# Layer B of a two-layer encoder: instructions that wait for another engine are issued one background share after their inputs

## The chip, the cores and the metric

The kernel runs on one core of one Trainium2 chip, in one launch. The metric is the device time of the execution in microseconds (us). The engines are PE (TensorE), DVE (VectorE), ACT (ScalarE), POOL (GpSimd) and SP (SyncE, which issues most DMAs). Each works through its own instructions in a fixed order, and the program makes it wait on semaphores for what other engines or DMAs produce.

## What is computed

Two layers run over 2048 prompt frames and 64 sample frames of width 1024:

```python
def gated_attention_layer(x_p, x_s, ck, cv, norm_g, w_in, q_g, k_g, w_out,
                          n_heads, n_kv, past_chunks, bias_fn, sinks):
    qp, kp, vp, gp = project(x_p, norm_g, w_in, q_g, k_g, n_heads, n_kv)
    op = prompt_band_attention(qp, kp, vp, past_chunks, bias_fn, sinks)
    y_p = x_p + (op * jax.nn.silu(gp)) @ w_out
    qs, ks, vs, gs = project(x_s, norm_g, w_in, q_g, k_g, n_heads, n_kv)
    os_, nk, nv = sample_band_attention(qs, ks, vs, ck, cv, bias_fn, sinks)
    y_s = x_s + (os_ * jax.nn.silu(gs)) @ w_out
```

`project` is an RMSNorm, one matrix product that gives queries, keys, values and gate, and an RMSNorm per head of 64 on queries and keys. The band is the own chunk of 64 frames and the past chunks. Layer A has 16 query heads on 2 key/value heads, 2 past chunks and sinks. Layer B has 16 heads, 8 past chunks and a learned bias by clipped distance. The outputs are the two results and the newest keys and values of both layers.

## The kernel before

Layer A takes the first part of the span (to about 690 us), its output projection follows, layer B lies between 876 and 2055 us, and its output projection ends the program. The change is to layer B.

Layer B goes through eight **head pairs**. In each it goes through units of 256 prompt frames (two tiles of 128) and one sample unit of 64. For a tile, `project` (L679 to L681) multiplies the normed input (fp16, in a high and a low part) by the head pair's 512 columns of weights into a PSUM bank `pj`: queries, keys, values and gate. `evacuate_b` takes it out: L715 (ACT) queries and keys into `pa`, L719 (ACT) the high half of the values, L720 (DVE) their low half, L723 (ACT) the gate into `pb`. The sample unit's bank is emptied by `evacuate_sample` (L740).

Then come small steps that change engines, each a **background item** in `bg`: `head_norm` squares (L756, POOL), sums (L757, DVE), adds and takes a power (L760, L761, POOL) and scales (L774, DVE); `gate` takes a tanh (L782, ACT) and multiplies (L783, DVE); `store_kv` scales the keys and stores (L795, POOL and SP). In the kernel before, squares, sums and power are one item, and tanh and product are one.

Attention works on what earlier projections left: queries and keys are transposed into the bank `tp` and taken out in a high half (L1355, L1356, ACT) and a low half (L1367 queries, L1371 keys, DVE); scores go into a bank `sb` (L1416, L1417); L1420 (DVE) adds the bias and takes the row's negative maximum `nm`; L1429 (ACT) is the exponential; L844 transposes the probabilities; L816 (ACT) and L817 (DVE) take them out as high and low half `ph` and `pl`; products (L1526 and L1527 for the sample unit) write the bank `o`. `finish_pairs` takes `o` out: L1247 (ACT) copies one half, L1249 (DVE) adds the other, L1250 (POOL) multiplies by the gate, L1252 (SP) stores.

The scan finds the largest magnitudes of the weights, from which powers of two for the fp16 scales follow: `scan` loads 128 x 512 weights (L182, SP) and reduces the block that it loaded a call before (L175, DVE). At the end of a head pair `across` transposes the maxima through `tp` (L197), and `everywhere` spreads the scales (L213 and the copy behind it). `load_weights` multiplies the weights by the scales (L467 ACT, L470 DVE).

**What sets the order.** PE's order is written out by hand: attention steps come due at marks of the projection's progress (`filler`), so that projection matmuls fill the time in which a step's inputs are made. At each attention step `bg.share` runs a share of the queue of background items, urgent items first. A background item's DVE and ACT instructions are tied behind the latest L1420 and L1429 (`anchor`), and each scan load behind the latest load of inputs (`behind`). The order of DVE, ACT, POOL and SP is otherwise left to the framework's scheduler, which goes by the order in which instructions are emitted and by when it reckons them ready. Banks of PSUM: two `pj`, one `tp`, two `sb`, one `o`.

Of the kernel before, what the change touches and what calls it, by code (L numbers as in the profile page):

```python
# [51 lines left out]
LAG = 4  # L52
HALF = 5 * 2 * P
# [3 lines left out]
def hybrid_encoder_kernel(  # L57
# [114 lines left out]
    def scan(i=None):  # L172
        if pending:
            j, raw = pending.pop()
            nc.vector.tensor_reduce(  # L175
                most[:, j : j + 1], raw, axis=AX.X, op=ALU.max, apply_absolute_value=True
            )
            scanned.append(j)
        if i is not None:
            raw = t("scan", [P, 512], 2)  # L180
# [12 lines left out]

    def across(a, b):
        ps = psum("tp", 512, 1)
# [14 lines left out]
    def everywhere(h, o):  # L210
        ps = psum("tp", 512, 1)
        nc.tensor.matmul(ps[:, 0:3], ones[0:1, 0:1].to_broadcast([1, P]), o, start=True, stop=True)
        nc.vector.tensor_copy(scl[:, h], ps[:, 0:3])  # L213
# [14 lines left out]
    def input_scales(h):  # L228
        everywhere(h, row[:, 20:23])
        nc.vector.tensor_scalar(gsb[:, h], gain[:, 1, :], S_W(h), 1.0, op0=ALU.mult, op1=ALU.mult)  # L230
# [25 lines left out]
    def scale_work(hp, u, e):  # L256
        at = 2 * u + e
        if hp < 7:
            if at < 8:
                scan(8 * (hp + 1) + at)  # L260
            elif at == 8:
                scan()
# [6 lines left out]
            if 11 <= at < 14 and i < 84:  # L269
                scan(i)  # L270
            elif at == 14:
                scan()
# [15 lines left out]
    def bias_vectors_a():  # L288
        oh = held["oh"]
        ps = psum("tp", 512, 1)  # L290
# [79 lines left out]
    class Background:  # L370
        def __init__(self):
            self.queue, self.anchors, self.cost, self.lazy = [], {}, 0.0, False

        def put(self, cost, fn, urgent=False, lazy=False, weights=False):
            it = Item()
            it.fn, it.cost, it.urgent, it.weights = fn, cost, urgent, weights
# [13 lines left out]
        def run(self, it):  # L390
            if it.fn is None:
                return
            fn, it.fn = it.fn, None
# [24 lines left out]
        def share(self, least, parts, few):  # L418
            left = sum(it.weights for it in self.queue)
            self.drain(max(least, self.cost / parts), 1 if left <= few else 2)  # L420

    bg = Background()

    def load_weights(g, *specs, scale=None):
        dt = F32R if scale is None else F16
# [80 lines left out]
    def load_act(  # L506
        src, o, T, squares=False, joint=False, lead=None, cache=None, cached=False, dt=F32R,
        rows=None, scale=None,
    ):
        x = Item()  # L510
# [123 lines left out]
    def token_rows(unit):  # L634
        _, T, tiles = unit
        ps = psum("tp", 512, 1)
# [75 lines left out]
    def evacuate_b(hp, tt, ps, g):  # L712
# [7 lines left out]
        nc.vector.scalar_tensor_tensor(  # L720
            vh[:, :, HD:P], v, c, vh[:, :, 0:HD], op0=ALU.mult, op1=ALU.subtract
        )
# [24 lines left out]
    def head_norm(n, src, spread=True):  # L747
# [3 lines left out]
        def squares():  # L751
            sq = t("sq", [P, 256], 2)
            f.append(t("f", [P, 4], 3))
            fv = f[0][:n, :H]
            if spread:
                nc.gpsimd.tensor_tensor(sq[:n, : H * HD], src, src, op=ALU.mult)  # L756
                nc.vector.tensor_reduce(  # L757
                    fv, sq[:n, : H * HD].rearrange("p (h d) -> p h d", d=HD), axis=AX.X, op=ALU.add
                )
                nc.gpsimd.tensor_tensor(fv, fv, small[:n, :H], op=ALU.add)  # L760
                nc.gpsimd.tensor_tensor(fv, fv, mhalf[:n, :H], op=ALU.pow)  # L761
                return
# [7 lines left out]

        def scale():
# [4 lines left out]
        return [bg.put(0.15 * H, squares, True), bg.put(0.1 * H, scale, True)]  # L776

    def gate(n, g):
        def fn():
            W = g.shape[1]  # L780
            e = t("sq", [P, 256], 2)
            nc.scalar.activation(e[:n, :W], g, AF.Tanh, scale=0.5)  # L782
            nc.vector.scalar_tensor_tensor(g, e[:n, :W], 1.0, g, op0=ALU.add, op1=ALU.mult)  # L783

        return [bg.put(0.3, fn)]
# [6 lines left out]
    def store_kv(layer, rows, kn, v, kdst, vdst):  # L792
# [9 lines left out]
        return bg.put(0.1, fn)  # L802
# [62 lines left out]
    class Filler:  # L865
# [9 lines left out]
        def step(self):  # L875
            if self.gen is None:
# [23 lines left out]
            if not self.attending:  # L900
                bg.drain(FR * c)
# [1027 lines left out]
```

## Time and profile before

| | |
|---|---|
| time, median of 3 runs | 2213.11 us (2212.63 to 2213.92) |
| the profiled execution | 2212.35 us, of it 2210.5 us in the span |
| mean granted clock of PE | 0.987 |
| busy over the span | PE 95%, DVE 70%, ACT 64%, POOL 45% |
| share of the chain that ended last | PE 58%, DVE 15%, DMA 9%, ACT 8%, issue 6%, POOL 4% |

A busy engine is one that executes; in the rest of the span it waits or has nothing to do. In the timeline a row has its start, its duration, engine, line, operation, output and inputs with their shapes, how many instructions it groups, and in brackets the idle time before it with what ended it. A row of waits has the waiting instruction, what it waited for, the total, how often, and the longest.

### The profile page before, as it was taken

The numbers are of one execution on the slowest core, as the hardware profiler recorded it, in microseconds if no ns is written. First come the engines' busy times: TensorE is split into PE (matmuls) and PEld (weight loads), VectorE is DVE, ScalarE is ACT, GpSimd is POOL, SyncE is SP. The second block draws the span as 40 slices with busy tenths as digits, with TensorE's granted clock in tenths as the row PEclk, the third lists the DMA queues.
The fourth block names the chain that finished last, engine by engine and source line by source line (L and its number), as shares of the span: only waits on it lengthen the run. The fifth ranks groups of instructions, "written<-read, shape, count | busy, mean of one in ns | idle before, by whom it ended". The sixth has DMA issues, their size and how long they took to land.

```text
span 2210.5 us, 41329 instructions
## 1 busy us (share of the span) xinstructions
PE 2110.9 (95%) x13441; PEld 1526.6 (69%) x13441; DVE 1547.2 (70%) x4105; ACT 1424.8 (64%) x3610; POOL 999.5 (45%) x1509
## 2 busy tenths in 40 slices
PE   7999999999999999999999989999999999998999
PEld 6877888787889997555555555555555555566888
DVE  6769777677676456787777776777767767577542
ACT  6878878677785333666666766766667667576420
POOL 5645544334355355853444444444444445443000
PEclk9999999999999999999999999999999999999999
DMA  8856546856545667445465565664646556345664
GB/s 276 275 160 215 180 125 220 229 164 182 180 128 178 216 192 256 158 143 172 117 180 136 128 178 133 160 167 115 196 118 162 158 118 171 95 105 136 198 202 124
DMA packets 383096, 372.87 MB, mean 169 GB/s; under 512 B 174672, under 2 KB 320352, under 8 KB 382848
## 3 DMA queue, kind: packets, MB, share of 16 engines
q1 hardware_dynamic: 382880, 370.23, 58.0%
q8 instruction: 106, 1.74, 0.3%
q14 instruction: 110, 0.90, 0.1%
HBM read 257.59 MB, written 73.43 MB: 150 GB/s over the span
## 4 chain that ended last, share of the span: by engine, by line
PE 58%; DVE 15%; DMA 9%; ACT 8%; issue 6%; POOL 4%; SPq 1%; POOLq 0%; ACTq 0%; DVEq 0%
PE pj L679 9%; PE pj L681 9%; PE pj L680 9%; PE pj L1772 4%; PE pj L1774 4%; PE pj L1773 4%; DMA scan<-in_w_in_b_dram 3%; DVE p L1420 3%; PE sb L844 2%; PE sa L844 2%; PE o L1607 2%; PE tp L844 2%; PE o L1568 2%; PE sb L1416 1%; ACT p L1429 1%
## 5 line engine op out<-in xcount | busy, mean ns | idle before, releaser
L679 PE MATMUL pj<-wh,xx 128*128 128x512 f16 (+2 forms) x1648 | 644.6, 391 | 5.2 <-ACT pb L702 3.9
L681 PE MATMUL pj<-wh,xx 128*128 128x512 f16 (+2 forms) x1648 | 626.4, 380 | 2.5 <-POOL xx L564 2.5
L680 PE MATMUL pj<-wh,xx 128*128 128x512 f16 x1024 | 392.0, 383 | 0.0
L1429 ACT ACTIVATE p<-p,nm 128x640 f32<-128x640 f32 (+5 forms) x264 | 199.2, 754 | 202.6 <-DVE nm L1420 102.4
L1772 PE MATMUL pj<-xx,wh 128*128 128x264 f32 (+1 forms) x1024 | 291.4, 285 | 8.0 <-DVE res L1778 2.7
L1773 PE MATMUL pj<-xx,wh 128*128 128x264 f32 (+1 forms) x1024 | 288.8, 282 | 0.0
L680 PE MATMUL pj<-wl,xx 128*128 128x512 f32 (+1 forms) x624 | 234.1, 375 | 2.2 <-DVE wl L470 2.2
L1420 DVE CUSTOM_DVE_ANT_0 p<-sb,BT 128x640 f32<-128x640 f32 (+5 forms) x272 | 195.7, 720 | 44.7 <-PE sb L1417 42.3
L564 POOL TENSOR_TENSOR xx<-xraw,xx 128x528 fp32r<-128x528 f32 (+4 forms) x144 | 183.8, 1295 | 88.9 <-ACT xx L563 82.1
L1464 POOL TENSOR_TENSOR values<-p,values 128x640 f16<-128x640 f32 (+2 forms) x112 | 141.2, 1261 | 159.4 <-ACT values L1463 158.8
L1250 POOL TENSOR_TENSOR o<-gt,o 128x256 f32<-128x256 f32 (+1 forms) x132 | 100.8, 763 | 207.7 <-DVE o L1249 96.8
L761 POOL TENSOR_TENSOR f<-f,mhalf 128x4 f32<-128x4 f32 (+2 forms) x187 | 187.5, 1003 | 13.7
L681 PEld LDWEIGHTS <-xx 128*128 128x128 f16 x1024 | 101.0, 99 | 126.4 <-issue 4.7
L756 POOL TENSOR_TENSOR sq<-pa 128x256 f32<-128x256 f32 (+2 forms) x187 | 113.1, 605 | 147.1 <-ACT pa L715 94.3
L1156 ACT ACTIVATE p<-p,nm 128x257 f32<-128x257 f32 (+2 forms) x272 | 134.3, 497 | 51.1 <-DVE nm L1150 42.9
L774 DVE TENSOR_TENSOR pa<-pa,f 128x256 f32<-128x256 f32 (+3 forms) x221 | 120.3, 544 | 57.9 <-POOL f L761 53.2
L679 PEld LDWEIGHTS <-xx 128*128 128x128 f16 x1024 | 101.3, 99 | 71.9 <-issue 3.1
L680 PEld LDWEIGHTS <-xx 128*128 128x128 f16 x1024 | 101.1, 99 | 70.1 <-issue 3.0
L1774 PE MATMUL pj<-xx,wl 128*128 128x264 f32 x512 | 145.7, 285 | 0.8 <-DVE wl L463 0.8
L1774 PE MATMUL pj<-xx,wh 128*128 128x264 f16 x512 | 142.7, 279 | 2.1 <-DVE wh L460 2.1
L1150 DVE CUSTOM_DVE_ANT_0 p<-sa,BT,nsink 128x256 f32<-128x256 f32 (+2 forms) x272 | 117.4, 467 | 36.0 <-PE sa L844 29.9
L679 PEld LDWEIGHTS pj<-wh,xx 128*128 128x128 f32 x624 | 118.7, 190 | 23.0 <-ACT pb L702 4.8
(273 smaller groups left out, 5276.9 us busy)
## 6 DMA issues: line engine op xcount, KB each, us to landing
xx<-xsb SPq DMA_DIRECT2D x112, 512.0 KB, 4.1
xx<-xsa SPq DMA_DIRECT2D x88, 512.0 KB, 4.8
xraw<-oga SPq DMA_DIRECT2D x64, 264.0 KB, 3.6
xraw<-ogb SPq DMA_DIRECT2D x64, 264.0 KB, 3.7
xsa<-xx SPq DMA_DIRECT2D x32, 512.0 KB, 4.1
scan<-in_w_in_b_dram SPq DMA_DIRECT2D x64, 256.0 KB, 4.5
wl<-in_w_in_b_dram SPq DMA_DIRECT2D x64, 256.0 KB, 4.1
xraw<-in_x_dram SPq DMA_DIRECT2D x40, 256.0 KB, 4.0
```

The lines of the kernel that those rows point to most:

```text
L564: nc.gpsimd.tensor_tensor(lo, rv, wide(hi), op=ALU.subtract)
L679: nc.tensor.matmul(ps[:n, :C], xh, wh, start=k == 0, stop=False)
L680: nc.tensor.matmul(ps[:n, :C], xh, wl, start=False, stop=False)
L681: nc.tensor.matmul(ps[:n, :C], xl, wh, start=False, stop=k == KC - 1)
L761: nc.gpsimd.tensor_tensor(fv, fv, mhalf[:n, :H], op=ALU.pow)
L1156: ex = nc.scalar.activation(pv[:n, h % 2, : nk + 1], pv[:n, h % 2, : nk + 1], AF.Exp, scale=-1.0, bias=nm[:n, h : h + 1], accum_out=sm[:n, ...
L1420: mi = nc.vector.tensor_tensor_reduce(out=p[r, :nk], in0=S[r, o : o + nk], in1=b, op0=ALU.add, op1=ALU.min, scale=1.0, scalar=3e38, accum_ ...
L1429: ex = nc.scalar.activation(p[:n, :nk], p[:n, :nk], AF.Exp, scale=-1.0, bias=it.nm[:n, c : c + 1], accum_out=it.sm[:n, c : c + 1],)
L1464: lo = nc.gpsimd.tensor_tensor(two[:, :, 1, :], pv, two[:, :, 0, :], op=ALU.subtract)
L1772: nc.tensor.matmul(ps[:, :OT], wh, oh, start=k == 0, stop=False)
L1773: nc.tensor.matmul(ps[:, :OT], wh, ol, start=False, stop=False)
L1774: nc.tensor.matmul(ps[:, :OT], wl, oh, start=False, stop=k == KC - 1)
```

## The change

It touches only where instructions stand; what is computed and PE's order stay.

- `head_norm` becomes three items in layer B: squares; sums and power; scale. `gate` becomes two: tanh; product. An item names another as `after`, and a share skips it if that one ran in the same share. `sq` has four buffers (it had two), `f` four (three).
- In `evacuate_b` the values' low half (L720) becomes an item, run at the latest before the next projection or output bank. The gate's evacuation (L723) is emitted without it.
- In `finish_pairs` the additions (L1249), the product and the store become an item (`held["ends"]`), run at the latest before the next `gate_t` or `o` bank. The copies (L1247) stay.
- In `everywhere` the copy of the scales and what is made from it become an item (`held["scales"]`), run at the latest before the next `tp` bank, weights or inputs.
- `scan` in layer B keeps one more load pending: a block is reduced two calls after its load was issued. Its buffers come from the three of `wraw`; `input_top` moves one call on.

```diff
-    def scan(i=None):
-        if pending:
-            j, raw = pending.pop()
+    def scan(i=None, keep=0):
+        while len(pending) > keep:
+            j, raw = pending.pop(0)
             nc.vector.tensor_reduce(
                 most[:, j : j + 1], raw, axis=AX.X, op=ALU.max, apply_absolute_value=True
             )
             scanned.append(j)
         if i is not None:
-            raw = t("scan", [P, 512], 2)
+            raw = t("wraw", [P, 512], WB) if keep else t("scan", [P, 512], 1)
...
+    def tp_bank():
+        run_all("scales")
+        return psum("tp", 512, 1)
+
+    def run_all(name):
+        while held[name]:
+            bg.run(held[name].pop(0))
...
     def everywhere(h, o):
-        ps = psum("tp", 512, 1)
+        ps = tp_bank()
         nc.tensor.matmul(ps[:, 0:3], ones[0:1, 0:1].to_broadcast([1, P]), o, start=True, stop=True)
-        nc.vector.tensor_copy(scl[:, h], ps[:, 0:3])
+
+        def fn():
+            nc.vector.tensor_copy(scl[:, h], ps[:, 0:3])
+            if h < 8:
+                nc.vector.tensor_scalar(gsb[:, h], gain[:, 1, :], S_W(h), 1.0, op0=ALU.mult, op1=ALU.mult)
+
+        held["scales"].append(bg.put(0.3, fn, True))
...
-                scan(8 * (hp + 1) + at)
+                scan(8 * (hp + 1) + at, 1)
             elif at == 8:
+                scan(None, 1)
+            elif at == 9:
                 scan()
                 input_top(hp + 1)
...
+                if it.after is not None and (it.after.fn is not None or it.after.tick == self.tick):
+                    continue
...
-        nc.vector.scalar_tensor_tensor(
-            vh[:, :, HD:P], v, c, vh[:, :, 0:HD], op0=ALU.mult, op1=ALU.subtract
-        )
+
+        def low():
+            nc.vector.scalar_tensor_tensor(
+                vh[:, :, HD:P], v, c, vh[:, :, 0:HD], op0=ALU.mult, op1=ALU.subtract
+            )
+
+        held["rest"].append(bg.put(0.2, low, True))
         held["evac"] = nc.scalar.activation(g, ps[:, 384:512], AF.Identity, scale=C_B(hp)).ins
...
-        return [bg.put(0.15 * H, squares, True), bg.put(0.1 * H, scale, True)]
...
+        first = bg.put(0.15 * H - 0.1 * apart, squares, True)
+        if not apart:
+            return [first, bg.put(0.1 * H, scale, True)]
+        second = bg.put(0.1 * H, sums, True, after=first)
+        return [first, second, bg.put(0.1 * H, scale, True, after=second)]
...
-        return [bg.put(0.3, fn)]
...
+        first = bg.put(0.2, curve)
+        return [first, bg.put(0.2, product, after=first)]
...
-        for hh, rows in enumerate(halves):
-            nc.vector.tensor_tensor(o1v[rows], Ov[0:64, :, hh, :], o1v[rows], op=ALU.add)
-        nc.gpsimd.tensor_tensor(o1v, gtv, o1v, op=ALU.mult)
-        if later:
-            held["later"].append(lambda: store(dst, o1v))
+
+        def fn():
+            for hh, rows in enumerate(halves):
+                nc.vector.tensor_tensor(o1v[rows], Ov[0:64, :, hh, :], o1v[rows], op=ALU.add)
+            nc.gpsimd.tensor_tensor(o1v, gtv, o1v, op=ALU.mult)
+            if key:
+                held["later"].append(last)
+            else:
+                store(dst, o1v)
+
+        def last():
+            store(dst, o1v)
+            finished[key] = finished.get(key, 0) + 1
+
+        if key:
+            held["ends"].append(bg.put(0.8, fn, True))
         else:
...
+        def o_bank():
+            run_all("rest")
+            run_all("ends")
+            return psum("o", 512, 1)
```

Rows of the order follow, with each kernel's own line numbers. The new lines are L176 for L175, L750 for L720, L803 for L757, L812 for L774, L832 for L783, L869 for L817, L1306 for L1249, L1436 and L1440 for L1367 and L1371, L1489 for L1420.

DVE at the sample unit of head pair 1 (1190 to 1194 us), before. `o_3098` is the output bank, `p_3108` the next masked scores, `scan_` (later `wraw_`) the block loaded by the scan:

```order
L175 TENSOR_REDUCE most_88<-scan_3164_15910 128x1
L1249 TENSOR_TENSOR o1_3101_15562<-o_3098_15514,o1_3101_15562 64x256 x2
L175 TENSOR_REDUCE most_88<-scan_3180_15993 128x1
L720 SCALAR_TENSOR_TENSOR values_2360_11645<-pj_3092_15493,values_2360_11645 128x2x64
L1420 ISA p_3108_15595,nm_3085_15467<-sb_3107_15594,BT_95 128x640
```

and now:

```order
L176 TENSOR_REDUCE most_88<-wraw_3164_15908 128x1
L1489 ISA p_3108_15590,nm_3085_15465<-sb_3107_15589,BT_95 128x640
L1489 ISA nm_3085_15465 128x1
L1306 TENSOR_TENSOR o1_3101_15561<-o_3098_15511,o1_3101_15561 64x256 x2
L750 SCALAR_TENSOR_TENSOR values_2360_11645<-pj_3094_15488,values_2360_11645 128x2x64
L176 TENSOR_REDUCE most_88<-wraw_3180_15991 128x1
```

The maximum with its second row has moved ahead of the additions, between them and the first reduce.

DVE ahead of "across" at the end of head pair 1 (1238 to 1243 us), before. `KA` and `KB` are the two halves of the keys:

```order
L1367 SCALAR_TENSOR_TENSOR q2_0_110<-tp_3215_16186,qf_82,q1_3216_16191 64x256
L1371 SCALAR_TENSOR_TENSOR KA_103<-tp_3215_16186,kf_83,KA_103 64x256
L774 TENSOR_TENSOR pa_3214_16181<-pa_3214_16181,f_3220_16205 128x256
L1249 TENSOR_TENSOR o1_3225_16235<-o_3212_16164,o1_3225_16235 64x256 x2
L1420 ISA p_3227_16249,nm_3201_16101<-sb_3226_16248,BT_95 128x640
L1420 ISA nm_3201_16101 128x1
L1367 SCALAR_TENSOR_TENSOR q2_0_110<-tp_3215_16186,qf_82,q1_3216_16191 64x256
L1371 SCALAR_TENSOR_TENSOR KB_104<-tp_3215_16186,kf_83,KB_104 64x256
```

and now:

```order
L1436 SCALAR_TENSOR_TENSOR q2_0_110<-tp_3215_16185,qf_82,q1_3216_16190 64x256
L1440 SCALAR_TENSOR_TENSOR KA_103<-tp_3215_16185,kf_83,KA_103 64x256
L1436 SCALAR_TENSOR_TENSOR q2_0_110<-tp_3215_16185,qf_82,q1_3216_16190 64x256
L1440 SCALAR_TENSOR_TENSOR KB_104<-tp_3215_16185,kf_83,KB_104 64x256
L1489 ISA p_3227_16244,nm_3201_16097<-sb_3226_16243,BT_95 128x640
L1489 ISA nm_3201_16097 128x1
L803 TENSOR_REDUCE f_3220_16205<-sq_3219_16204 128x4
L1306 TENSOR_TENSOR o1_3225_16233<-o_3212_16161,o1_3225_16233 64x256 x2
L1506 RECIPROCAL sm_3200_16096<-sm_3200_16096 128x4
```

The second pair of low halves follows the first; scale, sums, additions and the maximum stand behind it.

DVE after the sample unit's projection in head pair 2 (1276 to 1286 us), before. `pl` is the low half of the probabilities, the instructions on `pj` empty the sample unit's bank:

```order
L1420 ISA p_3322_16741,nm_3320_16739<-sb_3321_16740,BT_95 128x640
L1420 ISA nm_3320_16739 128x1
L774 TENSOR_TENSOR pa_3302_16653<-pa_3302_16653,f_3313_16706 128x256
L1425 TENSOR_SCALAR nm_3320_16739<-nm_3320_16739 128x1
L175 TENSOR_REDUCE most_88<-scan_3384_17096 128x1
L817 SCALAR_TENSOR_TENSOR pl_3317_16725<-sb_3329_16767,ph_3316_16724 128x5x128
L740 SCALAR_TENSOR_TENSOR pa_3323_16755<-pj_3308_16687,scl_90,res_3324_16756 64x128 x3
L740 SCALAR_TENSOR_TENSOR pb_3307_16686<-pj_3308_16687,scl_90,res_3324_16756 64x64 x2
L175 TENSOR_REDUCE most_88<-scan_3406_17223 128x1
```

and now:

```order
L1489 ISA p_3321_16735,nm_3319_16733<-sb_3320_16734,BT_95 128x640
L1489 ISA nm_3319_16733 128x1
L1494 TENSOR_SCALAR nm_3319_16733<-nm_3319_16733 128x1
L176 TENSOR_REDUCE most_88<-wraw_3383_17091 128x1
L812 TENSOR_TENSOR pa_3301_16648<-pa_3301_16648,f_3312_16698 128x256
L176 TENSOR_REDUCE most_88<-wraw_3406_17221 128x1
L869 SCALAR_TENSOR_TENSOR pl_3316_16715<-sb_3328_16762,ph_3315_16714 128x5x128
L772 SCALAR_TENSOR_TENSOR pa_3322_16750<-pj_3307_16679,scl_90,res_3323_16751 64x128 x3
```

The second reduce has moved ahead of `pl`, and the scale of `pa` behind the first reduce.

More of the change, by code (lines that the diff above doesn't have):

```diff
@@ L52 @@
 LAG = 4
+SQB = 4
 HALF = 5 * 2 * P
@@ L269, in scale_work @@
             if 11 <= at < 14 and i < 84:
-                scan(i)
+                scan(i, 1)
             elif at == 14:
+                scan(None, 1)
+            elif at == 15:
                 scan()
@@ L392, in run @@
                 return
+            if it.after is not None:
+                self.run(it.after)
+            it.tick = self.tick
             fn, it.fn = it.fn, None
@@ L509, in load_act @@
     ):
+        run_all("scales")
         x = Item()
@@ L790, in split_v, with store_kv @@
         nc.gpsimd.tensor_tensor(vt[:n, :, HD:P], sv, vt[:n, :, 0:HD].bitcast(F32), op=ALU.subtract)
-    def store_kv(layer, rows, kn, v, kdst, vdst):
+    def store_kv(layer, rows, kn, v, kdst, vdst, after=None):
         def fn():
@@ L800, in fn @@
                 store(vdst, v)
-        return bg.put(0.1, fn)
+        return bg.put(0.1, fn, after=after)
     KA = const([P, SEQ], "KA", F16)
@@ L1309, in gen @@
                     v, kn = pr[:n, 256:384], pr[:n, 128:256]
-                    it.todo += head_norm(n, pr[:n, 0:256]) + gate(n, it.gate[:n, e])
+                    norm = head_norm(n, pr[:n, 0:256], apart=True)
+                    it.todo += norm + gate(n, it.gate[:n, e], True)
                     if it is its[0] and e == 0:
@@ L1699, in pipeline @@
                 step += 1
+            run_all("ends")
             flush()
```

87 lines of the change are left out of this document (53 added, 34 removed).

## The prediction

> **What bounds the kernel now.** I read the page first, then the busy times by stretch, then TensorE's waits in layer B, then the timeline where the longest of these waits lie.
>
> ```profile
> PE 2110.9 (95%) x13441; PEld 1526.6 (69%) x13441; DVE 1547.2 (70%) x4105; ACT 1424.8 (64%) x3610; POOL 999.5 (45%) x1509
> ```
>
> That is the whole span; now eight stretches from 876 to 2055 us, which are layer B, summed:
>
> ```profile
> sum 1179.00, PE 1119.31 PEld 676.30 DVE 871.30 ACT 788.38 POOL 567.74; mean PE 139.91 PEld 84.54 DVE 108.91 ACT 98.55 POOL 70.97
> ```
>
> TensorE is busy for 1119.31 of 1179.00 us there. Its work and its order don't change, so the 59.7 us in which it stands still there are the most that the change can give back. What it stands still for (from 876 to 2055 us: total, times, longest):
>
> ```profile
> PE sb L844 <- DVE nm L1420: 13.6, 6, 2.7
> PE tp L197 <- DVE KB L1371: 6.7, 6, 3.8
> PE sb L1416 <- DVE nm L1420: 5.6, 6, 1.9
> PE sb L844 <- ACT p L1429: 5.5, 5, 1.4
> PE sb L844 <- DVE pl L817: 4.2, 9, 0.9
> PE tp L844 <- DVE pa L774: 2.0, 2, 1.5
> ```
>
> VectorE is named in 32.1 of these us: for the masked maximum L1420, the low halves of the keys L1371, the low half of the probabilities L817 and the norm's scale L774. It runs its instructions in order, and over the whole kernel these waits stand in its queue and in ScalarE's:
>
> ```profile
> DVE pa L774 <- POOL f L761: 53.2, 83, 1.7
> DVE most L175 <- DMA scan<-in_w_in_b_dram: 48.1, 25, 5.1
> DVE pb L783 <- ACT sq L782: 22.0, 33, 1.2
> ACT pb L723 <- DVE values L720: 44.0, 42, 3.5
> ```
>
> The change puts L774, L783 and L720 where their inputs are older. Lines here are those of the kernel before.
>
> **Part by part: "across".** Between two head pairs TensorE transposes the scan's maxima (L197) into the bank that the last L1371 releases.
>
> ```profile
> 1238.80 0.47 DVE L1367 SCALAR_TENSOR_TENSOR q<-tp,qf,q 64x256 f16<-64x256 f32 x1
> 1239.28 0.48 DVE L1371 SCALAR_TENSOR_TENSOR KA<-tp,kf,KA 64x256 f16<-64x256 f32 x1
> 1240.28 0.42 DVE L774 TENSOR_TENSOR pa<-pa,f 128x256 f32<-128x256 f32 x1 [0.52 <-POOL f L761]
> 1240.62 0.84 DVE L1249 TENSOR_TENSOR o<-o,o 64x256 f32<-64x256 f32 x2
> 1241.49 0.82 DVE L1420 CUSTOM_DVE_ANT_0 p<-sb,BT 128x640 f32<-128x640 f32 x1
> ...
> 1242.87 0.49 DVE L1371 SCALAR_TENSOR_TENSOR KB<-tp,kf,KB 64x256 f16<-64x256 f32 x1
> 1243.41 0.27 PE L197 MATMUL tp<-ident,top 128*1 128x128 f32 x1 [0.59 <-DVE KB L1371]
> ```
>
> In the new order the second L1367/L1371 pair follows the first, ahead of the scale, the additions and the maximum. It would end near 1239.76 + 0.98 = 1240.74, 2.1 us before TensorE is free (1243.41 - 0.59). Of the 6.7 us above five waits are of this kind, 6.7 - 3.8 = 2.9; I take **-2.7** (bounds -2.9 and 0). The longest stays.
>
> **L817.** Its nine waits sum to 4.2 us, none over 0.9. Ahead of it go mostly one L720 (0.28 us in a row below) and one L757 (0.41) or L774 (0.42): 0.6 to 0.8. I take **-3.2** (bounds -4.2 and 0, should the scores' high half on ScalarE end last).
>
> **The end of a head pair.** After the sample unit's projection the maxima wait longest. Head pair 2:
>
> ```profile
> 1276.90 0.96 SPq L182 DMA_DIRECT2D scan<-in_w_in_b_dram  x2
> 1282.63 0.69 DVE L175 TENSOR_REDUCE most<-scan 128x1 f32<-128x512 f32 x1 [5.07 <-DMA scan<-in_w_in_b_dram]
> 1283.24 0.81 DVE L817 SCALAR_TENSOR_TENSOR pl<-sb,ph 128x640 f16<-128x640 f32 x1
> ...
> 1285.55 0.69 DVE L175 TENSOR_REDUCE most<-scan 128x1 f32<-128x512 f32 x1
> ...
> 1289.21 1.43 DVE L783 SCALAR_TENSOR_TENSOR pb<-sq,pb 128x64 f32<-128x64 f32 x1
> ...
> 1296.06 1.27 DVE L470 SCALAR_TENSOR_TENSOR wh<-wl,gsb,wh 128x512 f16<-128x512 f32 x1 [0.16 <-ACT wh L467]
> 1297.26 0.62 DVE L774 TENSOR_TENSOR pa<-pa,f 128x256 f32<-128x256 f32 x1
> 1297.79 0.48 DVE L783 SCALAR_TENSOR_TENSOR pb<-sq,pb 128x128 f32<-128x128 f32 x1
> 1298.20 0.81 DVE L1420 CUSTOM_DVE_ANT_0 p<-sb,BT 128x640 f32<-128x640 f32 x1
> ...
> 1299.17 0.85 PE L844 MATMUL sb<-ident,p 128*128 128x128 f32 x5 [2.71 <-DVE nm L1420]
> ```
>
> The scan does not do here what the change says: both reduces still stand right behind their loads, the second now ahead of L817, which pays one reduce (from 1282.63 to L817 at 1283.24, 0.61 us). That delay is then swallowed by ScalarE, which works without a gap until the third maximum. At the end L774 and L783 leave the way of the last L1420: from L774's start to L1420's, 1298.20 - 1297.26 = 0.94. L470 ahead of it still waits for ScalarE, so no more than that is to be had. I take 0.9 at four head pairs, **-3.6** (bounds -4 x 2.7 and +4 x 0.6). In head pairs 1 and 6 the same waits for L1420 stand, and the additions L1249 (two of 0.42) step behind a maximum as well, but L817 or ScalarE is late next; **-1.5** (0 to -4).
>
> **The start of layer B.** Both of TensorE's waits for L774 lie here, 2.0 us, the longer one this:
>
> ```profile
> 902.79 0.44 PE L844 MATMUL tp<-ident,pa 128*128 128x128 f32 x2 [1.53 <-DVE pa L774]
> ```
>
> The squares are then summed and scaled in turns of their own, which leaves other work ahead of this place; **-1.5** (-2.0 to 0). Small waits at the end: **-0.5**. ScalarE's 44.0 us behind L720 are mostly not on the path: TensorE names L723 in none of the rows above; nothing taken.
>
> **What is added.** One output bank is shared by all of layer B's outputs. At the sample unit TensorE's L1526 begins just when the additions L1249 have emptied it:
>
> ```profile
> 1190.53 0.69 DVE L175 TENSOR_REDUCE most<-scan 128x1 f32<-128x512 f32 x1 [3.13 <-DMA scan<-in_w_in_b_dram]
> 1191.13 0.84 DVE L1249 TENSOR_TENSOR o<-o,o 64x256 f32<-64x256 f32 x2
> 1192.11 0.36 PE L1526 MATMUL o<-VS,ph 128*128 128x256 f32 x1
> 1192.60 0.28 DVE L720 SCALAR_TENSOR_TENSOR values<-pj,values 128x128 f16<-128x128 f32 x1
> 1192.80 0.81 DVE L1420 CUSTOM_DVE_ANT_0 p<-sb,BT 128x640 f32<-128x640 f32 x1
> ```
>
> In the new order L1420 stands between the reduce and L1249. Its scores are written by then, so the additions end some 0.75 us later (0.81 less some overlap with its successor), and the 0.14 us of slack (1191.13 + 0.84 = 1191.97, to 1192.11) covers little: about 0.65 at each of six head pairs, **+3.9** (0 to 4.9). A later scale copy and one more bank, **+0.5**.
>
> Sum: -2.7 - 3.2 - 3.6 - 1.5 - 1.5 - 0.5 + 3.9 + 0.5 = **-8.6 us**. The profiled execution took 2212.35 us (span 2210.5), 0.76 under the median of 2213.11; so 2203.75 there, and **2204.5** as a median. Under 0.2%, 4.4 us, a measurement can't tell a difference from none.
>
> **Rivals.** *The next engine is late (no change).* ScalarE's exponentials follow the maxima, and before L1429 the change also moves the gate's evacuation L723 forward. If ScalarE ends last wherever I counted L1420, only 2.7, 3.2, and 1.5 of the gains remain: -7.4 + 4.4 = -3.0, 2210. For it: 5.5 us in which L1429 is named already; against it: 19.2 us that name L1420.
>
> *The scan's loads hold more (slower).* VectorE now meets the second reduce before L817. Its load was issued by 1277.86, its reduce began only at 1285.55, and when it landed no row shows. If it landed just then, L817 comes 1285.55 + 0.61 - 1283.24 = 2.9 us later, at four head pairs: 11.6. At five other places SyncE now issues a transposition ahead of the scan's load:
>
> ```profile
> 1190.76 1.33 SPq L1472 DMA_TRANSPOSE pt<-values  x1
> ```
>
> and the load itself, from the page's DMA issues, takes 4.5 us to land:
>
> ```profile
> scan<-in_w_in_b_dram SPq DMA_DIRECT2D x64, 256.0 KB, 4.5
> ```
>
> 5 x 1.33 = 6.7 more. Then -8.6 + 18.3 = +9.7, 2223. It decides against the change from 13.0 us of added waiting over the nine places, 1.4 at each. Against it: with the median landing of 4.5 us the second load is in before the first reduce ends.
>
> *Products that meet GpSimd (no change).* Moved products can fall beside GpSimd's work, as one did already:
>
> ```profile
> 1289.16 1.40 POOL L1464 TENSOR_TENSOR values<-p,values 128x640 f16<-128x640 f32 x1
> ```
>
> L783 on 64 columns took 1.43 us beside it, against 0.48 on 128 columns at 1297.79. If one more such meeting, 0.95 us, lies ahead of a maximum at eight places, the gain shrinks by 7.6 to -1.0: 2212. The Trainium skill ("SBUF — State Buffer", section "Who interferes with whom") says that a VectorE instruction with two inputs in SBUF and a GpSimd instruction that reads SBUF exclude each other, and that the later one blocks; this trace agrees, as L783 ends (1290.64) when L1464 does (1290.56). Against this rival: at the places quoted the products now stand behind the maximum.
>
> *The scan's waits go after all (more gain).* Then neither the 3.9 nor the 0.6 at L817 is paid, and part of the 48.1 us comes back: about -13 - 7 = -20, 2193.
>
> **How the numbers follow.** My forecast (a gain of 4.4 to 14 us) 0.50; the next engine 0.16; the loads 0.20; GpSimd 0.08; more gain 0.06. Faster by over 0.2%: 0.50 + 0.06 = 0.56; within: 0.16 + 0.08 = 0.24; slower: 0.20. The range leaves out the largest gain and the worse half of the slower case, together under 0.2: 2197 to 2217; the forecast's own is 2199 to 2209.
>
> **What would show it.** Right: TensorE's waits for L1371 fall from 6.7 us to about 4 and those for L817 below 1.5; the 2.71 at the end of a head pair becomes about 1.8; new waits of some 0.65 us appear before L1526, named after L1249; ScalarE no longer waits for L720; VectorE's waits on the scan stay near 48 us. Wrong: waits for L817 over 1.5 us behind the second reduce, or waits of TensorE on ScalarE that grow by what L1420's lose.

## The result, and the profile after

The changed kernel takes 2215.59 us (median of 22 runs), the kernel before 2213.85 us beside it (22 runs): a ratio of 1.001, interval 0.9999 to 1.002. Run once more beside another 23 runs of before it gave 1.0015 (1.0002 to 1.0028). It is level or 2 to 3 us slower; forecast was 8.6 us faster. Single executions of either kernel scatter by some 3.5 us (standard deviation), so the experiments below lean on ratios and on stages of several profiles. The first profile of the changed kernel took 2213.74 us.

Page of the changed kernel, busy time, and then the sum of the eight stretches from 876 to 2055 us:

```profile
PE 2108.1 (95%) x13441; PEld 1525.1 (69%) x13441; DVE 1537.7 (70%) x4105; ACT 1425.8 (64%) x3610; POOL 1008.1 (46%) x1509
```

```profile
sum 1179.00, PE 1112.85 PEld 672.20 DVE 863.74 ACT 789.53 POOL 579.75; mean PE 139.11 PEld 84.02 DVE 107.97 ACT 98.69 POOL 72.47
```

These stretches begin at fixed times, and layer A ended 5 us later in this execution, so they hold a little less of layer B. What TensorE waits for says more (876 to 2055 us: total, times, longest; the rows that bear on the forecast; names and lines of the new file, L1489 for L1420, L869 for L817, L1440 for L1371, L1306 for L1249, L224 for L213):

```profile
PE sb L896 <- DVE pl L869: 7.1, 11, 1.9
PE sb L896 <- ACT sq L826: 6.3, 5, 1.3
PE sb L896 <- ACT p L1498: 5.4, 6, 1.1
PE tp L896 <- DVE scl L224: 5.3, 5, 1.1
...
PE o L1600 <- DVE o L1306: 4.5, 7, 0.8
PE tp L206 <- DVE KB L1440: 3.9, 1, 3.9
PE pj L1848 <- DVE wh L487: 3.6, 3, 1.7
...
PE sb L1485 <- DVE nm L1489: 2.9, 4, 0.7
...
PE sb L896 <- POOL G L1517: 2.4, 5, 1.3
...
PE sb L896 <- DVE nm L1489: 1.1, 2, 0.6
```

The waits that the forecast meant to remove are gone: five for the low keys (6.7 us to 3.9), those for the maxima (13.6 and 5.6 to 1.1 and 2.9, with 6.3 left at the ends of five head pairs, below). As many new ones stand beside them: output additions 4.5, scale copy 5.3 (1.3 before), the gate divided by the row's sum (G) 2.4, weight splits 3.6 (2.1 before), L869 7.1 (4.2 before). Matched instruction by instruction, TensorE's waits in layer B sum to 63.2, 66.9 and 67.2 us in three profiles of the kernel before, and to 65.5 and 65.7 in two of the changed one.

The sample unit of head pair 1 shows the forecast's one new wait as it was worked out, the additions a maximum later:

```profile
1196.22 0.81 DVE L1489 CUSTOM_DVE_ANT_0 p<-sb,BT 128x640 f32<-128x640 f32 x1
...
1196.96 0.84 DVE L1306 TENSOR_TENSOR o<-o,o 64x256 f32<-64x256 f32 x2
1197.95 0.36 PE L1600 MATMUL o<-VS,ph 128*128 128x256 f32 x1 [0.70 <-DVE o L1306]
```

The scale copy shows one that was not. Timeline before and after:

```profile
1252.15 0.16 DVE L213 COPY scl<-tp 128x3 f32<-128x3 f32 x1 [1.37 <-PE tp L212]
```

```profile
1256.44 0.38 PE L221 MATMUL tp<-scrow,ones 1*128 1x3 f32 x2
1257.32 0.43 DVE L812 TENSOR_TENSOR pa<-pa,f 128x256 f32<-128x256 f32 x1 [1.11 <-POOL f L807]
1257.66 0.15 DVE L224 COPY scl<-tp 128x3 f32<-128x3 f32 x1
1257.87 0.66 PE L896 MATMUL tp<-ident,pa 128*128 128x128 f32 x4 [1.05 <-DVE scl L224]
```

The scale of the norm, L812, is issued a share later so as to find its factor ready. It finds it not ready, stands still for 1.11 us, and the copy that was free to run waits behind it.

The end of head pair 2 (L1489 at 1303.51 is what TensorE needs, though the row names the tanh that ended last on ScalarE):

```profile
1302.22 0.18 DVE L1506 RECIPROCAL sm<-sm 128x4 f32<-128x4 f32 x1 [0.15 <-ACT p L1498]
1302.43 0.46 DVE L1509 TENSOR_SCALAR sm<-sm 128x2 f32<-128x2 f32 x1
1302.84 0.75 DVE L497 SCALAR_TENSOR_TENSOR wh<-wl,gsb,wh 128x512 f16<-128x512 f32 x1
1303.51 0.82 DVE L1489 CUSTOM_DVE_ANT_0 p<-sb,BT 128x640 f32<-128x640 f32 x1
...
1304.47 0.74 PE L896 MATMUL sb<-ident,p 128*128 128x128 f32 x5 [1.25 <-ACT sq L826]
```

The 2.71 us have become 1.25.

Waits of VectorE over the whole kernel, before:

```profile
DVE p L1420 <- PE sb L1417: 42.3, 50, 2.8
DVE pl L817 <- ACT ph L816: 34.1, 56, 2.9
```

and now:

```profile
DVE pl L869 <- ACT ph L868: 68.4, 76, 2.9
DVE p L1489 <- PE sb L1486: 68.0, 56, 5.9
DVE most L176 <- DMA wraw<-in_w_in_b_dram: 34.0, 21, 4.5
DVE pa L812 <- POOL f L807: 29.0, 60, 1.5
DVE most L176 <- DMA scan<-in_w_in_b_dram: 3.3, 4, 2.1
```

The scan's waits fell from 48.1 to 37.3 (34.0 + 3.3, in new buffers and the old one), the scale's from 53.2 to 29.0. Neither went away. ScalarE's 44.0 us behind L720 did. But both engines now stand still longer elsewhere: VectorE for the scores and for the high half of the probabilities, as the rows show, and ScalarE for the maxima that L1494 (L1425 before) hands it, 131.2 us against 77.0.

**By stage.** The scatter sits largely in layer A, whose order the change does not touch. So I took the time between the same TensorE instructions (the first ones behind 876, 1020, 1879 and 2055 us of the first profile) in four profiles of before's order (three of the kernel before, one of it with the change's buffers alone) and two of the changed kernel. The first row begins with TensorE's first instruction, the last ends with its last:

```
us                       before's order, 4 profiles      changed, 2     difference
to 876                   870.1  873.2  868.8  870.5     874.8  868.6      +1.0
876 to 1020 (first pair) 143.7  143.1  141.8  143.9     144.8  144.5      +1.5
1020 to 1879             861.2  863.2  864.6  861.8     856.5  858.5      -5.2
1879 to 2055 (last pair) 173.7  172.6  170.3  170.3     175.3  176.0      +3.9
2055 to the end          151.6  149.7  149.1  149.6     150.3  149.1      -0.3
```

The middle gains 5 us; the first and the last head pair give it back. In the middle TensorE's waits fall by 3.9 us, in the first and the last pair they rise by 2.0 and 1.9.

### The profile page after: what moved, and what is told of

Same layout as the page of the kernel before. It is cut to its first block, busy times and chain, and to the rows that moved or that the text cites. A ratio compares the mean times of both kernels' runs of the same rounds, so it can differ in the third digit from the quotient of the medians.

```text
span 2211.9 us, 41281 instructions
## 1 busy us (share of the span) xinstructions
PE 2108.1 (95%) x13441; PEld 1525.1 (69%) x13441; DVE 1537.7 (70%) x4105; ACT 1425.8 (64%) x3610; POOL 1008.1 (46%) x1509
## 4 chain that ended last, share of the span: by engine, by line
PE 56%; DVE 13%; ACT 11%; DMA 10%; issue 5%; POOL 3%; SPq 1%; ACTq 0%; POOLq 0%; DVEq 0%
PE pj L707 9%; PE pj L709 9%; PE pj L708 9%; PE pj L1846 4%; PE pj L1848 4%; PE pj L1847 4%; DMA wraw<-in_w_in_b_dram 3%; DVE p L1489 2%; PE sb L896 2%; PE sa L896 2%; ACT p L1498 2%; PE tp L896 2%; PE o L1680 2%; PE o L1642 1%; DVE pl L869 1%
## 5 line engine op out<-in xcount | busy, mean ns | idle before, releaser
L1498 ACT ACTIVATE p<-p,nm 128x640 f32<-128x640 f32 (+5 forms) x264 | 199.5, 756 | 238.0 <-DVE nm L1494 131.2
L1489 DVE CUSTOM_DVE_ANT_0 p<-sb,BT 128x640 f32<-128x640 f32 (+5 forms) x272 | 195.6, 719 | 71.4 <-PE sb L1486 68.0
L869 DVE SCALAR_TENSOR_TENSOR pl<-sb,ph 128x640 f16<-128x640 f32 (+4 forms) x144 | 106.1, 736 | 68.9 <-ACT ph L868 68.4
L806 POOL TENSOR_TENSOR f<-f,small 128x4 f32<-128x4 f32 (+2 forms) x187 | 45.9, 247 | 227.8 <-DVE f L803 222.7
L1848 PE MATMUL pj<-xx,wh 128*128 128x264 f16 x512 | 141.9, 277 | 3.6 <-DVE wh L487 3.6
L1204 DVE CUSTOM_DVE_ANT_0 p<-sa,BT,nsink 128x256 f32<-128x256 f32 (+2 forms) x272 | 117.4, 468 | 38.8 <-PE sa L896 31.6
```

The lines of the kernel that those rows point to most:

```text
L1489: mi = nc.vector.tensor_tensor_reduce(out=p[r, :nk], in0=S[r, o : o + nk], in1=b, op0=ALU.add, op1=ALU.min, scale=1.0, scalar=3e38, accum_ ...
L1498: ex = nc.scalar.activation(p[:n, :nk], p[:n, :nk], AF.Exp, scale=-1.0, bias=it.nm[:n, c : c + 1], accum_out=it.sm[:n, c : c + 1],)
L1848: nc.tensor.matmul(ps[:, :OT], wl, oh, start=False, stop=k == KC - 1)
```

## The experiments

Three theories stood against each other: that each deferral has a bill of its own; that a removed wait only lets the next one show; that the added buffers slow layer A. Times are against the kernel before on the same chip, as ratio and interval.

**The changed kernel again** (no edit).

> The changed kernel once more, unaltered. Theory 1 (the 7 us by which layer A was late in its first profile are scatter between executions, since the order of layer A's instructions has not changed): the offset against the profile of before at 650 us differs from +7.0 by 2 us or more, and what the eight head pairs add from 1180 to 1880 us repeats to 0.5 us (it was +4.95 to +1.09, so -3.9). Theory 2 (the change itself slows layer A, by its buffers): +7 again at 650 us. Time within 0.2% of before by both.

Ratio 1.0015 (1.0002 to 1.0028). At 650 us it stands 2.1 us ahead of the first profile of before, where the first one stood 7.0 behind: scatter. The stretch from 1180 to 1880 us adds -2.0 us (-3.9 in the first), so that part repeats less closely than expected.

**Scale copy at once.**

```diff
-        held["scales"].append(bg.put(0.3, fn, True))
+        fn()
```

> The changed kernel with the scale copy and what is made of it issued at once, as before. Theory 1 (each deferral has its own bill: the scale copy 5 waits of 0.8 us more, 4.0 in all): the five waits of TensorE for the scale copy fall from 1.05 to about 0.25 us each and the time falls by about 4 us against the changed kernel. Theory 2 (these waits only take up slack that the next wait would have taken): the waits fall, the next wait (that for L817 before unit 7, 0.44) grows by as much, and the time stays.

1.0008 (0.9996 to 1.002). The five waits stay at 5.3 us. Both theories had the wrong culprit: it is not the copy's own deferral that makes it late.

**Output additions at once.**

```diff
-            held["ends"].append(bg.put(0.8, fn, True))
+            fn()
```

> The changed kernel with the output additions, gate product and store issued at once, as before. Theory 1: the waits before L1526 (7 of about 0.65 us, 4.5 in all) vanish, but the additions stand ahead of the maximum and of the key halves again, so that some of the 3.7 us gained at across come back as waits: net -1 to -4 us against the changed kernel. Theory 2 (the deferral earns what it costs): net within 1 us.

1.0047 (1.0031 to 1.0063): slower, against both expectations. The waits before L1526 vanish, but:

```profile
PE sb L896 <- DVE pl L869: 21.2, 29, 1.6
PE sb L1485 <- DVE nm L1489: 8.3, 15, 1.5
```

L869 rose from 7.1 to 21.2 us and L1489 in front of the scores from 2.9 to 8.3. Why additions at once cost so much beside the other parts, and not in the kernel before, was not traced.

**Both at once** (the two edits together).

> Both of the former at once. Theory 1: the bills are separate, so the gains add: 5 to 8 us under the changed kernel, about 2207 to 2210 us where before has 2213 to 2214. Theory 2: under 2 us.

1.0039 (1.0024 to 1.0054): as with the additions at once, within the intervals, and against both expectations too.

**The kernel before again**, for two more profiles.

> The kernel before once more, unaltered, for a second profile. Theory 1 (the sums of TensorE's waits are set by the order and repeat, while clock and DMAs scatter): the waits of layer B sum to the same within 1.5 us (63.3 us in the rows of 876 to 2055 us), and the time of layer B differs from the first profile's by more than that where the granted clock differs.

> The kernel before a third time, one look, for a profile. Both profiles so far (2212.35 and 2213.21 us) lie above the median of the runs beside the experiments (2208.9), so that layer B may be some 3 to 4 us shorter in a usual execution than in them. Theory 1 (those were long executions): layer B, 1006 us and 1007 us in the two, takes 1001 to 1004 us in an execution of 2207 to 2210 us. Theory 2 (layer B is as long always, and the scatter sits in layer A and the two output projections): 1006 us whatever the time.

2213.21 and 2206.50 us. Waits in layer B are 66.9 and 67.2 us, 3.7 and 4.0 above the first profile, so they repeat less well than expected. From 876 to 1879 us the three took 1004.9, 1006.4 and 1006.4 us: theory 2 of the third, this stretch is as long in a short execution as in a long one.

**Norm and gate whole.**

```diff
     def head_norm(n, src, spread=True, apart=False):
+        apart = False
...
     def gate(n, g, apart=False):
+        apart = False
```

> The changed kernel with norm and gate in one piece again (squares, sums and power in one item; tanh and product in one). Theory 1 (the scale L812, which now comes a share later, is what stands ahead of the scale copy and ahead of the maximum in front of unit 7): the five waits for the scale copy fall from 1.05 to 0.25 us, 4.0 in all, those for L869 at unit 7 (five of 0.44 to 0.53) vanish, 2.3; what the split had earned (waits for L774 at the start of layer B, 2.0, part of those for L817) comes back: net -2 to -5 us against the changed kernel. Theory 2 (the deferred low half of the values and the deferred additions made these waits): they stay within 0.3 us of the changed kernel, and the time within 1 us.

1.0021 (1.001 to 1.0032), no faster than the changed kernel. The waits for the scale copy do fall, from 5.3 to 1.3 us: the split is shown as their cause, and the timeline above names L812. The five waits for L869 in front of unit 7 do not vanish (0.3 to 0.5 us each), so theory 1 had their cause wrong. They are gone in both kernels with the additions at once. The waits before L1526 grow to

```profile
PE o L1602 <- DVE o L1308: 10.4, 7, 2.2
```

and those for L869 to 12.5 us, at other places.

**Low half at once**, run twice.

```diff
-        held["rest"].append(bg.put(0.2, low, True))
+        low()
```

> The changed kernel with the values' low half issued at once, ahead of the gate's evacuation, as before. Theory 1: ScalarE waits for it again (some 44 us over 42 places), off the path at most of them: 0 to +2 us against the changed kernel. Theory 2 (the early gate evacuation, which now stands ahead of the exponential, costs 0.3 us at each of four head pairs): -1 us.

> The changed kernel with the values' low half issued at once, a second time. Theory 1 (the deferred low half was the dearest part of the change, 6 to 7 us): 4 to 5 us under the kernel before again. Theory 2 (chance): within 1 us of the kernel before.

0.9983 (0.9971 to 0.9994) and 0.999 (0.9979 to 1.0001): some 2 to 4 us faster than before, though the second interval takes in no difference. Both theories of the first run had it slower or no more than 1 us under the changed kernel; the second lies between its two. 1020 to 1879 us took 852.6 and 849.5 us. In the waits of the second run L869 has 4.2 us (7.1 in the changed kernel), the scale copy 2.8 (5.3).

**Scan as before** (one load pending, two buffers of its own).

```diff
     def scan(i=None, keep=0):
+        keep = 0
...
-            raw = t("wraw", [P, 512], WB) if keep else t("scan", [P, 512], 1)
+            raw = t("scan", [P, 512], 2)
```

> The changed kernel with the scan as before (one load pending, two buffers of its own). Theory 1 (the reduces stand behind their loads either way; of the bill only the wait for the second reduce ahead of L869, 0.44 us at head pair 2, is the scan's): VectorE's waits for the scan stay at 45 to 52 us, the time within 1.5 us of the changed kernel. Theory 2 (the scan's new places hold back the maximum before the additions, and so make the 4.5 us before L1526): these waits fall below 1 us, -3 to -4 us.

1.0008 (0.9996 to 1.0019), about the changed kernel's. VectorE waits 38.8 us for the scan; with the changed scan it was 37.3, and 41.4 in the second profile, and 48.1 before. The fall is not the changed scan's doing, and theory 1 expected none. The waits before L1526 are 5.1 us, so theory 2 falls.

**Low half deferred, alone.** Every other part as before, but for the buffers.

> The kernel before with nothing of the change but the deferred low half of the values (and the numbers of buffers). Theory 1 (it costs by itself, since its place behind the maximum holds back the products and the projection's bank): 3 to 7 us over the kernel before. Theory 2 (it costs only together with the split norms, whose items it pushes back in the queue): within 1.5 us of the kernel before, ScalarE's 44 us of waits gone.

0.998 (0.9968 to 0.9992): faster, where both theories had level or slower. The same edit that costs inside the change gains outside it. At the ends of head pairs 2 to 5 TensorE's wait, 2.7 us before and 1.25 in the changed kernel, is 0.26 here.

**Split norms and deferred additions only** (low half, scale copy and scan as before).

> The changed kernel with low half, scale copy and scan as before, which leaves the split norms and gates and the deferred additions. Theory 1 (the parts' bills add: 6.7, 0.9 and 1.9 us were measured under the changed kernel): 8 to 9 us under the changed kernel, some 6 under the kernel before, 2202 to 2204 us. Theory 2 (they overlap): as with the low half alone, 4 us under the kernel before.

0.9979 (0.9967 to 0.9991): theory 2, overlapping.

**Four parts by themselves.**

> The kernel before with four buffers for the squares (two) and four for the norms' factors (three), and the code of the change with every deferral off; the order of all engines is that of before. Theory 1 (buffers cost nothing): within 1 us of before, waits of layer B at 63 to 67 us. Theory 2 (they move addresses or waits in layer A): +2 us or more, in layer A, which took 633.7 us on average over three profiles of before and 635.9 over eleven of the other kernels.

> Norm and gate in their pieces, nothing else deferred. Theory 1 (the scale's new place ahead of other work costs by itself): 5 us or more over before, with the waits for the scale copy at 1.05 us each and many waits for L869, as in the kernel with the additions at once, which was 11 us over. Theory 2 (that loss came from the low half beside the split): within 2 us of before.

> The output additions deferred, nothing else. Theory 1 (they clear the maxima and key halves and pay before L1526): the waits for L1371 fall by 2.8 us, those before L1526 appear with 4 to 6 us, the time within 2 us of before. Theory 2 (they are a loss by themselves): 3 us or more over before, as the kernel with norms whole (5 us over).

> Low half and additions deferred, norm, gate, scale copy and scan as before. Theory 1 (the deferred items crowd each other: all are urgent items of one queue, run in turn, so that the additions come later behind the low half): 3 to 6 us over before with waits before L1526 above 6 us, though the low half alone gained 4. Theory 2 (bills add): 4 us under before plus what the additions alone give.

Buffers 1.0001 (0.999 to 1.0013): theory 1, and layer A is cleared. Split 1.0008 (0.9994 to 1.0021): theory 2, though the five waits for the scale copy are 0.72 us each, against 0.25 before. Additions 1.0013 (1.0001 to 1.0025), 3 us over: between the theories. Low half with additions 1.0032 (1.0021 to 1.0043), slower though its half alone gained 0.2%: theory 1. The last two have waits before L1526 of 10.2 and 10.5 us, and a longest of 2.0 and 2.2 us each.

**The change in head pairs 1 to 6 only.**

```diff
-        held["rest"].append(bg.put(0.2, low, True))
+        if hp in MIDDLE:
+            held["rest"].append(bg.put(0.2, low, True))
+        else:
+            low()
```

and likewise for norm, gate, additions and scale copy, `MIDDLE = range(1, 7)`.

> The change in head pairs 1 to 6 only: norm, gate, low half, additions and scale copy are issued as before in the first and the last head pair (the scan is the changed one throughout). Theory 1 (the loss is made by what is deferred in the first and the last head pair): 876 to 1020 us takes 143 us and 1879 to 2055 us takes 171 to 172 us as before, the stretch between them 857 us against 863, the time 4 to 6 us under the kernel before. Theory 2 (the loss follows the work that the middle leaves behind, since queues and buffers carry over): the last stretch stays at 175 us or more, the time within 2 us of before.

0.9994 (0.9981 to 1.0007), median 2205.77 beside 2207.33. By stage 140.6, 854.4 and 173.5 us: the first head pair is back at before's time or better, the middle keeps its gain, the last stretch gives back half of its loss. The total cannot be told from before, so theory 1 has the stages for it more than the time, and these are of one profile, the shortest execution of this kernel (2198.55 us).

**The same with the low half at once everywhere.**

> As the former, with the low half at once everywhere. Theory 1 (stages add: 850 us in the middle, as with the low half at once, and before's first and last stretch): 9 to 11 us under the kernel before, 2197 to 2200 us. Theory 2: as the low half at once in the whole layer, 3 to 4 us under before.

2199.25 us against 2207.33, **0.9955 (0.9937 to 0.9973)**: the fastest version tried, 8 us under the kernel before, where theory 1 had 9 to 11. Stages 141.9, 851.1, 173.1 us, again of the shortest execution; the last remains above before's. Waits from 1018 to 1868 us:

```profile
PE sb L900 <- ACT p L1502: 6.2, 5, 1.4
PE o L1604 <- DVE o L1310: 5.0, 5, 1.3
...
PE sb L900 <- DVE pl L873: 3.5, 7, 1.9
PE sb L900 <- DVE nm L1493: 3.2, 5, 1.0
...
PE tp L900 <- DVE scl L225: 2.9, 5, 0.9
```

## Why the prediction was wrong

The step that failed is the one from waits removed to time gained. The forecast counted what leaves the way of the instructions that TensorE waits for, and allowed 4.4 us for all that enters it. About as much entered as left: TensorE's waits in layer B went from 63.2 to 65.5 us, where the forecast had 8.6 us less. By stage it missed at the start of layer B and at its end. Term by term, the first two profiles matched instruction by instruction:

*Across* (-2.7): right, five waits gone, -2.8.

*L817* (-3.2): the nine waits counted lost 3.9 us, but 6.8 us of waits for it arose at ten other places, 2.2 of them at the start of layer B (7.1 in all): +2.9. What failed is the count of what leaves the way of L817 without the count of what enters it.

*The end of a head pair* (-3.6): 2.7 became 1.25 at three of the four, more than the 0.9 counted; the fourth had 1.05 in this profile (2.72 in the later ones) and has 1.25: -4.2. L783 left with L774, and the contended L470 (1.27) became a plain one (0.75). The delay of L817 by the second reduce shows at head pair 2 alone, where the wait behind it went from 1.07 to 1.51 us. With the low half deferred alone 0.26 us is left here, and 0.56 in the changed kernel with the low half at once, so the parts hinder each other.

*Head pairs 1 and 6* (-1.5): right in direction. Three waits for L1420 of 1.88, 2.19 and 2.19 us became one of 1.25 and one of 1.85 for L869 (counted above): -3.2 with it.

*The additions before L1526* (+3.9): right, 4.5, of it 3.7 in five waits at sample units.

*A later scale copy* (in the +0.5): mis-sized. It cost 4.0 in five waits. The +0.5 had no working. Elsewhere the prediction counted what stands ahead of an instruction as busy time alone; here L812 brought 1.11 us of waiting beside its 0.43. The sentence that the change puts L774 "where its inputs are older" held for some of its places only.

*The start of layer B* (-1.5) *and small waits at the end* (-0.5): the terms that decided, with the wrong sign: those stages grew by 1.5 and 3.9 us. Without them the sum was -6.6, and the middle measured -5.2. That it came so near is partly luck: waits gave 3.9 us of it, and the rest is time of the matmuls, which the forecast took as fixed. Of the two terms the first named the waits that go and nothing that comes, the second named no place. At the start both waits for L774 go, and one of 1.9 us for L869 comes:

```profile
907.55 0.28 DVE L869 SCALAR_TENSOR_TENSOR pl<-sb,ph 128x128 f16<-128x128 f32 x1
...
910.65 0.48 DVE L1436 SCALAR_TENSOR_TENSOR q<-tp,qf,q 64x256 f16<-64x256 f32 x1 [1.26 <-ACT KB L1425]
...
912.65 0.42 DVE L869 SCALAR_TENSOR_TENSOR pl<-sb,ph 128x256 f16<-128x256 f32 x1
913.13 0.33 PE L896 MATMUL sb<-ident,p 128*128 128x128 f32 x1 [1.90 <-DVE pl L869]
```

The low halves of queries and keys, which in the middle profit from standing early, wait here for ScalarE and hold L869 back; before, L817 stood between the two pairs. This wait is not the whole of it: with the low half at once it is gone, and this stage took 148.2 and 146.3 us. At the end, where the output projection's weights are made, new waits stand at

```profile
1999.10 0.77 PE L896 MATMUL sb<-ident,p 128*128 128x128 f32 x5 [1.06 <-ACT p L1498]
2007.39 0.29 PE L1846 MATMUL pj<-xx,wh 128*128 128x264 f16 x1 [1.30 <-ACT wh L486]
2009.45 0.29 PE L1848 MATMUL pj<-xx,wh 128*128 128x264 f16 x1 [1.66 <-DVE wh L487]
```

VectorE has L832 (0.92), L812 (0.41) and other deferred items ahead of L487. These waits replace ones of 2.33 and 1.47 us; the sum of waits rises there by 1.6 to 2.2. The rest of the 3.9 is time of the matmuls, and goes with the clock (below): by it this stage lost 6.1, 5.1, 1.7 and 1.7 us in the four profiles of before's order and 4.9 and 6.8 in the two of the changed kernel, which is not clear of scatter.

*The rivals*: "the next engine is late", which forecast no change, had nearly the right result, mostly by luck. TensorE's waits for the exponential were 5.5 us and are 5.4; one new one, 1.06 at 1999.10, stands behind the gate's evacuation, which now comes first. VectorE itself stays the commonest cause. The scan's loads did not grow dearer. Products did meet GpSimd on the path: ahead of L487 L832 took 0.92 us, against 0.28 two us earlier, beside a GpSimd product that ended 0.15 us before it. But the kernel before has such a meeting at this place too (L774, 1.62 us), and over layer B the products did not get longer (L774 and L812 525 and 524 ns on average, L783 and L832 469 and 450), so this rival is not the cause.

What stays open: the two changed profiles and the four of before's order differ by less in sum (+0.9 us) than the medians do (+1.7 and +3.5), which is within the scatter; how much of the last head pair's loss is waits and how much clock; and why the low half gains alone, costs with the additions and costs with the whole change was seen only in where waits of VectorE come to stand, not traced to one scheduling decision.

## What to carry to other kernels

An instruction that is issued later is not off the path: it stands ahead of something else, and if its input is late there too, the wait moves with it. Count for each place in an order what enters ahead of the critical instruction, its wait included, and give the stages at both ends of a loop their own rows. Where a scheduler orders the engines, parts of a change do not add: try them alone and in pairs, and by stage.

## What the runs showed of the hardware

A wait of TensorE can cost more than its length. In the kernel with low half and additions deferred, after 1.87 us:

```profile
1762.93 0.35 PE L1599 MATMUL o<-VS,ph 128*128 128x256 f32 x1 [1.87 <-DVE o L1305]
...
1764.16 0.42 PE L706 MATMUL pj<-wh,xx 128*128 128x512 f16 x1
1764.38 0.63 PE L704 MATMUL pj<-wh,xx 128*128 128x512 f16 x1
1764.81 0.63 PE L705 MATMUL pj<-wh,xx 128*128 128x512 f16 x1
...
1767.58 0.48 PE L706 MATMUL pj<-wh,xx 128*128 128x512 f16 x1
1767.90 0.38 PE L704 MATMUL pj<-wh,xx 128*128 128x512 f16 x1
```

```profile
1760.00:1770.00 10.00, 8.13 (x37) 4.21 (x36) 7.62 (x22) 4.77 (x14) 3.28 (x6) 0.83 0.67 138
```

From 1764.4 on matmuls of 512 columns start 0.43 us apart (0.21 before), for 3.4 us; the granted clock of the slice is 0.83, a loss of 10 x 0.17 = 1.7 us. Here it comes 1.4 us after the wait's end. In twenty profiles, between 1020 and 1995 us, the recorded clock shows such a stretch at 0 of 456 waits of 0.3 to 1 us, 5 of 192 up to 1.45, 2 of 23 up to 1.8, 12 of 36 up to 2.4, 9 of 16 up to 3 and 18 of 20 longer ones (it begins after the wait's start and at most 3.4 us after its end; of two waits the longer counts).

What decides is where the wait falls. In each profile the clock changes only at points of a fixed grid, 3.41 us apart. All 30 grid intervals of which TensorE's waits took 60% or more (2.05 us) were followed by one at half rate, 20 of 131 with 40 to 60%, and 2 of 5529 with less. So the same wait can be followed or not. In the third profile of the kernel before:

```profile
1437.86 0.74 PE L844 MATMUL sb<-ident,p 128*128 128x128 f32 x5 [2.72 <-DVE nm L1420]
1579.16 1.11 PE L844 MATMUL sb<-ident,p 128*128 128x128 f32 x5 [2.72 <-DVE nm L1420]
```

```profile
1435.00:1445.00 10.00, 7.28 (x48) 4.60 (x48) 9.09 (x19) 6.62 (x15) 5.87 (x8) 1.00 0.67 229
1576.00:1586.00 10.00, 7.28 (x39) 4.29 (x37) 8.62 (x18) 6.34 (x15) 5.89 (x9) 0.83 0.66 232
```

The first straddled two intervals (the fuller had 54%), the second lay in one (80%); the granted clocks are 1.00 and 0.83.

In the middle the four profiles of before's order have 4, 4, 3 and 3 such stretches, nine of them at the waits of 2.7 us, and two of the changed kernel 1 and 2. With 1.7 us each that would be 3.4 of the 5.2 us that the middle gained. This is an estimate and too much: waits fell by 3.9 us there too, and the time of the matmuls without waits by 1.6 only. The kernel with low half and additions deferred has five, three of them right behind L1526, and is slower than before although its waits sum to less (61.5 us). The prediction priced waits by length alone, and took the 59.7 us of idle time as the most to be had.

The Trainium skill ("TensorE: Matmul & The Clock Gate", section "HAM oscillation — how this bites in real kernels") gives as rule of thumb to have no idle gaps over about 3.4 us, and puts the window of idleness that brings the slower clock at about that length. The runs agree on the half rate and on the length of the interval; as a limit for gaps 3.4 us is too long here, since one in three waits of 1.8 to 2.4 us was followed by it.
